# Weight sums of the second MLP product: started behind the first product's weight loads, and two of the four made by transfers that add

## The chip, the cores and the metric

One core of one Trainium2 chip. The metric is the device time of one execution in microseconds; the time of a kernel is the median of its runs. A profile shows one execution, whose own time is given beside its span.

## The reference

A hybrid decoder block on 512 tokens (and 16 meta tokens) of width 1024: two token mixers side by side (gated linear attention and an S5 state-space layer), merged by gates, and then an MLP with a squared ReLU. The change touches the MLP alone:

```python
hn = rmsnorm(h, g_ffn_pre[l])
f = jnp.square(jax.nn.relu(hn @ w_ff1[l])) @ w_ff2[l]
h = h + rmsnorm(f, g_ffn_post[l])
```

w_ff1 is 1024 x 4096 and w_ff2 is 4096 x 1024, in float32.

## The kernel before

Every matmul is made of three: a float32 operand is split into a high part (float32r, made by ACT at line 152, `whi`) and the rest (made by DVE at line 165, `wlo`), and hi x hi, hi x lo and lo x hi are summed in PSUM.

**First product.** w_ff1 is taken in 32 tiles of 128 columns. One tile is a 512 KB load on the SP queue (line 158, `wraw`, three buffers), a split into `whi` and `wlo` (three buffers each), 24 matmuls of 128x128 by 512 tokens into one PSUM bank of four, a ReLU by ACT (line 1251) and a square by DVE (line 1252) into `f`. The first three tiles are begun early and in two halves; the loop `for m in range(EARLY, MF)` runs over the other 29. After every fourth tile DVE makes sums of parts of `f` (`early_sums`).

**Second product.** It is done by a scheme with seven products of half size instead of eight (Strassen and Winograd's): sums of quarters of `f` are multiplied by quarters of w_ff2 or by sums of them. The four kinds of sums of w_ff2's quarters are made while the first product runs, in 16 steps, j = 0 to 15 (`weight_sums`). Step j loads 256 rows of w_ff2 (1 MB, `w2raw`, two buffers), makes four differences of 128x512 each on DVE into `w2t` (two buffers), and writes them (1 MB) to a tensor in HBM, `td2` (named t2d in the profile). Both transfers are issued by POOL. Call a step's two row blocks A and B, and their left and right halves l and r; then the four are

- t0 = Ar - Al
- t1 = Br - t0
- t2 = Br - Ar
- t3 = Bl - t1

The second product's sub-products read w_ff2 or td2 in 512 KB pieces on SP (line 1286) and begin when the first product is over; the second of them is the first that reads td2.

**Order.** A planner sets the order of the instructions in each engine's queue when the program is built, from the data dependences, the free buffers and a model of costs; at run time each queue is worked off in that order. `tc.issue_after(x)` makes the instructions of a block that are on x's engine come after x in that engine's queue; it adds no wait between engines. `behind()` is `issue_after` of the last load kept in `loaded`. In the stretch before the loop PE's order is the written one (`pinned`), in the loop it is the planner's.

Of the kernel before, what the change touches and what calls it, by code (L numbers as in the profile page):

```python
# [11 lines left out]
AF = mybir.ActivationFunctionType  # L12
ALU = mybir.AluOpType
# [3 lines left out]
P = 128  # L17
D = 1024
KT = D // P
SEQ = 512  # L20
# [8 lines left out]
MF = DFF // P  # L29
# [20 lines left out]
def hybrid_block(ctx: ExitStack, tc: tile.TileContext, io, out: bass.AP):  # L50
    nc = tc.nc
    V, S, G = nc.vector, nc.scalar, nc.gpsimd
# [18 lines left out]
    def mk(pool, shape, dt=F32, tag=None, **kw):  # L71
        count[0] += 1
        name = f"{tag or 'x'}_{count[0]}"
        size = 1
        for n in shape[1:]:
            size *= n
        if pool not in lined or size % LINE == 0:
            return pool.tile(shape, dt, tag=tag or name, name=name, **kw)
        t = pool.tile([shape[0], -(-size // LINE) * LINE], dt, tag=tag or name, name=name, **kw)[:, :size]
        if len(shape) == 2:  # L80
            return t
        dims = " ".join("abcd"[: len(shape) - 1])
        return t.rearrange(f"p ({dims}) -> p {dims}", **dict(zip("abcd", shape[1:])))

    def f32(t):
        return t.bitcast(F32)

    def pool(name, bufs=1, space=None, stack=None, side="left", padded=False):
        kw = {"side": side} if space is None else {"space": space}
        if space != DRAM:  # L90
            kw["reuse_waits"] = "tile"
        made = (stack or ctx).enter_context(tc.tile_pool(name=name, bufs=bufs, **kw))
        if padded:
            lined.append(made)
        return made
# [25 lines left out]
    def bank(tag="sm"):  # L121
        return mk(ps_mm if tag == "mm" else ps_sm, [P, 512], tag=tag)
# [28 lines left out]
    def split_hi(dst, src, scale=1.0):  # L151
        S.activation(dst, src, AF.Copy, scale=scale)  # L152

    def raw_w(src):

        kt, n = src.shape[0] // P, src.shape[1]
        raw = mk(wp, [P, kt, P], tag="wraw", bufs=3)
        return nc.sync.dma_start(raw[:, :, :n], src.rearrange("(k p) n -> p k n", p=P)), raw

    def split_w(raw):  # L160
        kt = raw.shape[1]
        hi = mk(wp, [P, kt, P], F32R, tag="whi", bufs=3)
        lo = mk(wp, [P, kt, P], F32R, tag="wlo", bufs=3)
        split_hi(hi, raw)
        V.tensor_sub(lo, raw, f32(hi))  # L165
        return hi, lo

    def load_w(src):

        return [split_w(raw_w(src[:, c : c + P])[1]) for c in range(0, src.shape[1], P)]  # L170

    def mm3(ps, whi, wlo, xhi, xlo, kt):

        for k in range(kt):
            PE.matmul(ps, whi(k), xhi(k), start=(k == 0), stop=False)
            PE.matmul(ps, whi(k), xlo(k), start=False, stop=False)
            last = PE.matmul(ps, wlo(k), xhi(k), start=False, stop=(k == kt - 1))
        return last

    def feat_tile(w, xh, xl, c0, c1, ps, m=P, kt=KT):  # L180
        hi, lo = w
        return mm3(ps, lambda k: hi[:, k, :m], lambda k: lo[:, k, :m], lambda k: xh[:, k, c0:c1], lambda k: xl[:, k, c0:c1], kt)
# [77 lines left out]
    loaded = None  # L260

    def behind():
        return tc.issue_after(loaded.ins) if loaded else ExitStack()

    def x_load(t):
        xt = mk(pxt, [P, D], tag="xt", bufs=5)
        xts.append((xt, P, t * P))
        return nc.sync.dma_start(xt, io["x"][0, t * P : (t + 1) * P, :])


    for kind, i in (("x", 0), ("x", 1), ("u", 0), ("x", 2), ("u", 1), ("x", 3)):
        with behind():
            if kind == "x":
                loaded = x_load(i)
            else:
                loaded, raw = raw_w(w_in[:, C_U + i * P : C_U + (i + 1) * P])
# [11 lines left out]
    for i in range(2):  # L288
        ps = bank()
# [5 lines left out]
    for i, (xt, n, col) in enumerate(xts):  # L295
        sq = mk(pxt, [P, D], tag="xsq", bufs=2)
        squared = S.activation(sq[:n], xt[:n], AF.Square, accum_out=ss[:n, i : i + 1])
# [18 lines left out]
    ps = bank()  # L316
# [781 lines left out]
    for c in range(0, D, 256):  # L1098
        ss_ = []
        for i, w in enumerate(load_w(wg[:, D + c : D + c + 256])):  # L1100
            m = c // P + i
            ps = bank("mm")
# [7 lines left out]
        for i, w in enumerate(load_w(wg[:, c : c + 256])):  # L1110
            m = c // P + i
            ps = bank("mm")
# [18 lines left out]
    for k in range(KT):  # L1131
        raw = mk(wp, [P, D], tag="wraw", bufs=3)
# [19 lines left out]
    hh = mk(pf, [P, KT, SEQ], F32R, tag="hh")  # L1152
    hl = mk(pf, [P, KT, SEQ], F32R, tag="hl")
# [48 lines left out]
    EARLY = 3  # L1202
    w1 = io["w_ff1"][0]
    w2 = io["w_ff2"][0]
# [10 lines left out]
    f = mk(pff, [P, MF, SEQ], tag="f")  # L1215
# [3 lines left out]
    NJ = MF // 2  # L1219
# [9 lines left out]
    def early_sums(jj):  # L1229

        a11, a12, a21, a22 = quarters(jj)
        V.tensor_add(s1[:, 2 * jj : 2 * jj + 2], a21, a22)
        V.tensor_sub(a21, a11, a21)

    spw = ExitStack()
    pw2 = pool("pw2", stack=spw)

    def weight_sums(j):

        raw = mk(pw2, [P, 2, D], tag="w2raw", bufs=2)  # L1240
        nc.gpsimd.dma_start(raw, w2[2 * j * P : (2 * j + 2) * P, :].rearrange("(k p) n -> p k n", p=P))  # L1241
        t_ = mk(pw2, [P, 4, 512], tag="w2t", bufs=2)
        V.tensor_sub(t_[:, 0], raw[:, 0, 512:], raw[:, 0, :512])  # L1243
        V.tensor_sub(t_[:, 1], raw[:, 1, 512:], t_[:, 0])  # L1244
        V.tensor_sub(t_[:, 2], raw[:, 1, 512:], raw[:, 0, 512:])  # L1245
        V.tensor_sub(t_[:, 3], raw[:, 1, :512], t_[:, 1])  # L1246
        nc.gpsimd.dma_start(td2[:, j].rearrange("i p n -> p i n"), t_)  # L1247

    def relu2(m, ps):
        r_ = mk(pff, [P, SEQ], tag="relu", bufs=2)  # L1250
        S.activation(r_, ps, AF.Relu)
        V.tensor_mul(f[:, m], r_, r_)

    for w, ps in zip(ws, pss):
        feat_tile(w, hh, hl, 256, 512, ps[:, 256:])
    pinned[0] = False
    for m, ps in enumerate(pss):
        relu2(m, ps)
    for m in range(EARLY, MF):
        ps = bank("mm")  # L1260
        feat_tile(load_w(w1[:, m * P : (m + 1) * P])[0], hh, hl, 0, SEQ, ps)
        relu2(m, ps)
        if m % 4 == 3:
            early_sums(m // 4)
        if m % 2 == 0:
            weight_sums(m // 2 - 2)
    for j in (NJ - 2, NJ - 1):
        weight_sums(j)
    spw.close()
    sf.close()  # L1270

# [137 lines left out]
```

## Time and profile before

| | |
|---|---|
| median of 3 runs | 909.98 us (909.49 to 912.02) |
| profiled execution | 909.35 us, span 907.6 us |
| granted TensorE clock | 0.996 of full speed |
| PE busy | 888.8 us, 98% of the span |
| DVE busy | 669.0 us, 74% |
| ACT busy | 407.6 us, 45% |
| POOL busy | 85.2 us, 9% |
| loop over the first product's 29 tiles | 585.4 to 746.8 us of the span |
| weight sums: first load issued, last write issued | 569.9 us, 696.0 us |

In the profile, a line such as "676.93 0.69 DVE L1243 TENSOR_TENSOR w2t<-w2raw ..." gives the start, the duration, the engine, the line of the kernel, the operation and the tiles written and read; in brackets stands how long the engine sat idle before it, and what ended that. A row of the busy time by stage gives the stretch, its length, the busy time of PE, PE's weight loads, DVE, ACT and POOL with their instructions in parentheses, the granted clock, the mean busy share of the 16 DMA engines, and GB/s. A row of a DMA queue gives its packets, MB, and the time of its packets as a share of the 16 engines' time. "DMA to landing" is the time from a transfer's issue to its end.

### The profile page before, as it was taken

To read this page: it belongs to the slowest core of one execution; us is meant where nothing else is said; L and a number is where in the kernel's file an instruction comes from. 1 tells how busy PE (TensorE), PEld (TensorE's weight loads), DVE (VectorE), ACT (ScalarE), POOL (GpSimd) and SP (SyncE) were. 2 spreads that over 40 slices of the span, in tenths; PEclk is the share of its full clock that TensorE was granted. 3 is DMA by queue.
4 is the path that set the end of the run, shared out by engine and by line. 5 is a ranking of instruction groups with operands and counts; after the bars stand their busy time and mean duration, and the time that the engine had idled before them with its cause. 6 is when DMAs were issued, how large, how long until landed. Compare 5 with 4: busy or idle time off the path is not lost.

```text
span 907.6 us, 13464 instructions
## 1 busy us (share of the span) xinstructions
PE 888.8 (98%) x4980; PEld 759.2 (84%) x4980; DVE 669.0 (74%) x1203; ACT 407.6 (45%) x667; POOL 85.2 (9%) x160
## 2 busy tenths in 40 slices
PE   7999999999999999999999999999999999999996
PEld 5899899898988888888888888988877888888885
DVE  7779998877877699876344765667766348778786
ACT  6362355556563434224223544432322326665762
POOL 1311100010101201103000000111120000000000
PEclk9999999999999999999999999999999999999999
DMA  7733644344435536367654672599999437655564
GB/s 231 184 107 120 198 107 116 101 122 113 109 105 141 159 100 193 107 193 261 185 152 148 215 191 70 180 358 377 392 377 320 128 100 272 208 188 202 167 209 139
DMA packets 172147, 166.68 MB, mean 184 GB/s; under 512 B 22397, under 2 KB 137153, under 8 KB 172082
## 3 DMA queue, kind: packets, MB, share of 16 engines
q1 hardware_dynamic: 155920, 110.48, 41.7%
q0 software_dynamic: 14480, 50.56, 14.8%
q10 hardware_dynamic: 1682, 4.79, 1.6%
q8 instruction: 39, 0.64, 0.3%
q14 instruction: 26, 0.21, 0.1%
HBM read 131.42 MB, written 34.37 MB: 183 GB/s over the span
## 4 chain that ended last, share of the span: by engine, by line
PE 83%; DMA 7%; issue 4%; DVE 4%; POOL 1%; ACT 0%; DVEq 0%; POOLq 0%
PE mm L60 59%; PE sm L60 21%; DMA w2raw<-in_w_ff_dram 6%; PE sm L65 3%; DVE xl L193 1%; DVE xn L302 0%; DVE w2t L1243 0%; POOL t2d L1247 0%; DMA xt<-in_x_dram 0%; DVE w2t L1244 0%; DVE wlo L165 0%; DVE w2t L1246 0%; DVE c L1352 0%; POOL w2raw L1241 0%; DVE w2t L1245 0%
## 5 line engine op out<-in xcount | busy, mean ns | idle before, releaser
L152 ACT ACTIVATE whi<-wraw 128x1024 fp32r<-128x1024 f32 x160 | 168.5, 1056 | 242.6 <-PE mm L60 174.7
L60 PE MATMUL mm<-xh,whi 128*128 128x512 f32 (+2 forms) x544 | 184.1, 338 | 0.5 <-DVE xl L193 0.5
L60 PE MATMUL mm<-xl,whi 128*128 128x512 f32 (+2 forms) x544 | 180.0, 331 | 0.5 <-DVE xl L193 0.5
L60 PE MATMUL mm<-xh,wlo 128*128 128x512 f32 (+2 forms) x544 | 180.0, 331 | 0.0
L165 DVE TENSOR_TENSOR wlo<-wraw,whi 128x1024 fp32r<-128x1024 f32 x104 | 126.9, 1221 | 56.5 <-ACT whi L152 51.8
L60 PEld LDWEIGHTS mm<-xh,whi 128*128 128x128 f32 x544 | 104.2, 192 | 11.3 <-issue 1.2
L60 PEld LDWEIGHTS mm<-xl,whi 128*128 128x128 f32 x544 | 104.2, 192 | 9.2 <-DVE xl L193 0.8
L60 PEld LDWEIGHTS mm<-xh,wlo 128*128 128x128 f32 x544 | 104.1, 191 | 9.1
L60 PE MATMUL mm<-hh,wlo 128*128 128x512 f32 (+1 forms) x280 | 104.3, 373 | 2.5 <-DVE wlo L165 2.5
L60 PE MATMUL mm<-hh,whi 128*128 128x512 f32 (+1 forms) x280 | 104.1, 372 | 0.2 <-ACT hh L152 0.2
L60 PE MATMUL mm<-hl,whi 128*128 128x512 f32 (+1 forms) x280 | 104.0, 371 | 0.3 <-DVE hl L193 0.3
L1289 DVE TENSOR_TENSOR wlo<-wraw,whi 128x1024 fp32r<-128x1024 f32 x56 | 68.4, 1222 | 23.0 <-ACT whi L152 23.0
L60 PE MATMUL sm<-wlo,fh 128*128 128x512 f32 x192 | 74.8, 390 | 0.0
L60 PE MATMUL sm<-whi,fh 128*128 128x512 f32 x192 | 74.7, 389 | 0.0
L60 PE MATMUL sm<-whi,fl 128*128 128x512 f32 x192 | 74.7, 389 | 0.0
L60 PEld LDWEIGHTS mm<-hh,wlo 128*128 128x128 f32 x280 | 52.7, 188 | 13.0 <-DVE wlo L165 4.1
L60 PEld LDWEIGHTS mm<-hl,whi 128*128 128x128 f32 x280 | 52.7, 188 | 9.7 <-DVE hl L193 0.5
L60 PEld LDWEIGHTS mm<-hh,whi 128*128 128x128 f32 x280 | 52.7, 188 | 9.4 <-ACT hh L152 0.5
L152 ACT ACTIVATE fh<-f 128x512 fp32r<-128x512 f32 x48 | 30.1, 629 | 44.0 <-PE sm L60 25.9
L60 PE MATMUL mm<-gl,whi 128*128 128x512 f32 x128 | 49.8, 389 | 0.0
L60 PE MATMUL mm<-gh,whi 128*128 128x512 f32 x128 | 49.8, 389 | 0.0
L60 PE MATMUL mm<-gh,wlo 128*128 128x512 f32 x128 | 49.8, 389 | 0.0
(409 smaller groups left out, 1562.1 us busy)
## 6 DMA issues: line engine op xcount, KB each, us to landing
wraw<-in_w_ff_dram SPq DMA_DIRECT2D x56, 512.0 KB, 4.9
wraw<-in_w_in_dram SPq DMA_DIRECT2D x48, 512.0 KB, 4.2
w2raw<-in_w_ff_dram POOLq DMA_DIRECT2D x16, 1024.0 KB, 9.6
t2d<-w2t POOLq DMA_DIRECT2D x16, 1024.0 KB, 7.5
wraw<-t2d SPq DMA_DIRECT2D x32, 512.0 KB, 3.7
wraw<-in_w_glu_dram SPq DMA_DIRECT2D x16, 512.0 KB, 3.8
M<-kpad SPq DMA_DIRECT2D x64, 64.0 KB, 2.5
wraw<-in_w_o_gla_dram SPq DMA_DIRECT2D x8, 512.0 KB, 4.5
```

The lines of the kernel that those rows point to most:

```text
L60: ins = nc.tensor.matmul(*args, **kw)
L65: ins = nc.tensor.transpose(*args, **kw)
L152: S.activation(dst, src, AF.Copy, scale=scale)
L165: V.tensor_sub(lo, raw, f32(hi))
L193: V.tensor_sub(lo[:, dst, col : col + n], pv[:, :, :n], f32(hi)[:, dst, col : col + n])
L1289: V.tensor_sub(bl, raw, f32(bh))
```

## The change

- Step j's load of w_ff2 rows moves from POOL's queue to SP's, and stands there behind the load of a tile of w_ff1: tile 3 + floor(28 j / 16), so that the 16 steps are spread over tiles 3 to 29. Before, they were written every second tile, and the planner ran them as their buffers came free.
- t0 and t2 are no longer made by DVE. ACT writes -Al and -Ar (copies with a scale of -1), and a transfer issued by POOL adds Ar and Br to them, read from w_ff2 in HBM a second time (512 KB).
- t1 and t3 stay on DVE, and are put behind the squaring of the tile that follows; the write to td2 follows them. Step j is a generator: its first part ends at `yield`, its second part is run one tile later.
- `w2t` has three buffers instead of two. `relu2` returns its last instruction, so that others can be put behind it.

```diff
     def weight_sums(j):
         raw = mk(pw2, [P, 2, D], tag="w2raw", bufs=2)
-        nc.gpsimd.dma_start(raw, w2[2 * j * P : (2 * j + 2) * P, :].rearrange("(k p) n -> p k n", p=P))
-        t_ = mk(pw2, [P, 4, 512], tag="w2t", bufs=2)
-        V.tensor_sub(t_[:, 0], raw[:, 0, 512:], raw[:, 0, :512])
+        rows = w2[2 * j * P : (2 * j + 2) * P, :].rearrange("(k p) n -> p k n", p=P)
+        nc.sync.dma_start(raw, rows)
+        t_ = mk(pw2, [P, 4, 512], tag="w2t", bufs=3)
+
+        S.activation(t_[:, 0], raw[:, 0, :512], AF.Copy, scale=-1.0)
+        S.activation(t_[:, 2], raw[:, 0, 512:], AF.Copy, scale=-1.0)
+        nc.gpsimd.dma_start(t_[:, 0:4:2], rows[:, :, 512:], accum_op=ALU.add)
+        yield
         V.tensor_sub(t_[:, 1], raw[:, 1, 512:], t_[:, 0])
-        V.tensor_sub(t_[:, 2], raw[:, 1, 512:], raw[:, 0, 512:])
         V.tensor_sub(t_[:, 3], raw[:, 1, :512], t_[:, 1])
         nc.gpsimd.dma_start(td2[:, j].rearrange("i p n -> p i n"), t_)
...
+    j, begun = 0, []
     for m in range(EARLY, MF):
         ps = bank("mm")
-        feat_tile(load_w(w1[:, m * P : (m + 1) * P])[0], hh, hl, 0, SEQ, ps)
-        relu2(m, ps)
+        loaded, raw = raw_w(w1[:, m * P : (m + 1) * P])
+        w = split_w(raw)
+        feat_tile(w, hh, hl, 0, SEQ, ps)
+        squared = relu2(m, ps)
         if m % 4 == 3:
             early_sums(m // 4)
-        if m % 2 == 0:
-            weight_sums(m // 2 - 2)
-    for j in (NJ - 2, NJ - 1):
-        weight_sums(j)
+        for part in begun:
+            with tc.issue_after(squared.ins):
+                next(part, None)
+        begun = []
+
+        while j < NJ and EARLY + j * (MF - EARLY - 1) // NJ <= m:
+            with behind():
+                begun.append(weight_sums(j))
+                next(begun[-1])
+            j += 1
+    for part in begun:
+        next(part, None)
```

More of the change, by code (lines that the diff above doesn't have):

```diff
@@ L1251, in relu2 @@
         S.activation(r_, ps, AF.Relu)
-        V.tensor_mul(f[:, m], r_, r_)
+        return V.tensor_mul(f[:, m], r_, r_)
     for w, ps in zip(ws, pss):
```

## The prediction

> **What bounds the kernel now.** I read the page's share of engines first, then the waits of PE in the stretch of the change (575 to 750 us), then busy time by stage, then the timeline around PE's gaps, then the POOL queue.
>
> ```profile
> PE 888.8 (98%) x4980; PEld 759.2 (84%) x4980; DVE 669.0 (74%) x1203; ACT 407.6 (45%) x667; POOL 85.2 (9%) x160
> ...
> PE mm L60 <- DVE wlo L165: 2.5, 3, 1.0
> ...
> 585.00:665.00 80.00, 80.00 (x356) 66.31 (x356) 58.74 (x85) 23.41 (x31) 16.14 (x22) 1.00 1.02 367
> 665.00:690.00 25.00, 22.49 (x96) 17.38 (x95) 17.14 (x25) 6.19 (x8) 5.18 (x7) 1.00 1.03 370
> 690.00:746.00 56.00, 56.00 (x249) 46.37 (x248) 28.02 (x34) 16.99 (x22) 0.76 (x1) 1.00 0.49 153
> ```
>
> PE is the bound, and it stalls in this stage at one place only: between 665 and 690 us it is busy for 22.49 of 25.00 us. There the DMA engines are full (share 1.03), as they have been since 585 us; afterwards they are half idle (0.49). The granted clock is 1.00 throughout. So the most that this edit can win is what these stalls cost. Two matmuls of one kind, 24 apart, give the undisturbed tile; the first matmul of the loop over the first product's tiles and the first of the second product give the stage.
>
> ```profile
> 639.85 0.39 PE L60 MATMUL mm<-hh,whi 128*128 128x512 f32 x1
> 645.29 0.39 PE L60 MATMUL mm<-hh,whi 128*128 128x512 f32 x1
> ...
> 585.42 0.40 PE L60 MATMUL mm<-hh,whi 128*128 128x512 f32 x1
> 746.84 0.39 PE L60 MATMUL sm<-whi,fh 128*128 128x512 f32 x1
> ```
>
> A tile takes 5.44 us, so 29 tiles take 157.8 us; they took 746.84 - 585.42 = 161.4 us. The stage loses **3.7 us** (2.5 us as waits, the rest as slower matmuls just behind each gap). Now what PE waits for:
>
> ```profile
> 676.93 0.69 DVE L1243 TENSOR_TENSOR w2t<-w2raw 128x512 f32<-128x512 f32 x1 [2.35 <-DMA w2raw<-in_w_ff_dram]
> 677.54 0.69 DVE L1245 TENSOR_TENSOR w2t<-w2raw 128x512 f32<-128x512 f32 x1
> 678.14 0.68 DVE L1244 TENSOR_TENSOR w2t<-w2raw,w2t 128x512 f32<-128x512 f32 x1
> 678.86 0.69 DVE L1246 TENSOR_TENSOR w2t<-w2raw,w2t 128x512 f32<-128x512 f32 x1
> 679.47 1.22 DVE L165 TENSOR_TENSOR wlo<-wraw,whi 128x1024 fp32r<-128x1024 f32 x1
> ...
> 680.74 0.50 PE L60 MATMUL mm<-hh,wlo 128*128 128x512 f32 x1 [0.95 <-DVE wlo L165]
> ```
>
> DVE waits for a weight-sum load (w2raw), does its four sums, and only then the low half (wlo) of the tile for which PE stands still. The order of DVE's queue is fixed, so a late weight-sum load holds up the first product.
>
> How late comes from a loop of two buffers: the load for sum j+2 cannot start before sum j's last subtraction frees its w2raw.
>
> ```profile
> 666.65 0.78 POOL L1247 DMA_DIRECT2D t2d<-w2t  x1 [7.16 <-DVE w2t L1246]
> 667.42 0.70 POOL L1241 DMA_DIRECT2D w2raw<-in_w_ff_dram  x1
> 673.14 0.78 POOL L1247 DMA_DIRECT2D t2d<-w2t  x1 [5.03 <-DVE w2t L1246]
> ...
> 679.85 0.78 POOL L1247 DMA_DIRECT2D t2d<-w2t  x1 [5.24 <-DVE w2t L1246]
> ```
>
> From 666.65 to 679.85 one turn takes 13.2 us (write issued, load issued 0.77 us later, 9.5 us to the first subtraction, 2.6 us of subtractions, hand-over), hence 6.6 us per sum. The queue order has about one sum per 5.44 us tile here, so DVE falls behind by about 1.2 us per sum until its lead is gone. That lead is worked out from how early the next weights are split when nothing disturbs:
>
> ```profile
> 730.49 1.06 ACT L152 ACTIVATE whi<-wraw 128x1024 fp32r<-128x1024 f32 x1 [3.90 <-PE mm L60]
> ```
>
> With three buffers the split of tile m+3 starts when tile m ends, and takes 1.06 us here and 1.22 us on DVE; PE needs it two tiles (10.9 us) later. Lead: 10.9 - 2.3 = 8.6 us, or some seven sums at 1.2 us each, which is about where the stall at 667 to 687 us lies.
>
> **The change, part by part.**
>
> *Pacing.* Sum j now starts behind the load of tile 3 + 28j/16, so there are 16 sums in 28 tiles: one in 1.75 tiles, 9.5 us, and a turn of two buffers may last 19.0 us where it now takes 13.2. The closing subtractions come behind the squaring of the following tile. Last sum: tile 29, closed behind tile 30 (about 743 us), written by some 752 us. Its readers:
>
> ```profile
> L1286 SPq DMA_DIRECT2D wraw<-t2d x12: 359/360/367, 759.8 to 787.8; - x12
> ```
>
> The first read (759.8 us) wants sums 0 and 1, the last pair is read much later: nothing is late there.
>
> *The new turn.* Taken out: two of four subtractions (0.6 us apart, 1.2 us) and the load's place behind the write on POOL (0.77 us, against 0.36 us of issue on SP, the row just above: 0.4 us). Put in: two ACT copies, one more POOL issue (0.78 us, rows above), and the adding transfer's time to landing, A. The nearest copy:
>
> ```profile
> L152 ACT ACTIVATE fh<-f 128x512 fp32r<-128x512 f32 x48 | 30.1, 629 | 44.0 <-PE sm L60 25.9
> w2raw<-in_w_ff_dram POOLq DMA_DIRECT2D x16, 1024.0 KB, 9.6
> t2d<-w2t POOLq DMA_DIRECT2D x16, 1024.0 KB, 7.5
> DMA to landing us min/median/max: 6.0/9.6/11.6
> DMA to landing us min/median/max: 3.8/7.9/14.6
> ```
>
> (The last two rows are from the views of tile w2raw and of line 158, the first product's loads of 512 KB.) Two copies: 1.3 us. New turn: 13.2 - 1.2 - 0.4 + 1.3 + 0.8 + A = 13.7 + A if the load still needs 9.5 us, and 10.2 + A if it lands in the least time seen, 6.0 us. It now shares no queue with the 1 MB write ahead of it, and sums come at 9.5 instead of 6.6 us; against that it stands behind 512 KB loads on SP. I take the middle, 11.9 + A.
>
> No transfer of before adds. Bounds for A: 512 KB plain and undisturbed, 3.8 us; twice the bytes under load, 7.5 to 9.6 us. I take 5.6 us, the middle of 3.8 and 7.5, since the bytes are nearest to the former and the load on the engines to the latter. Turn: 17.5 us, below 19.0: DVE no longer falls behind and PE's waits go, **-3.7 us**. At A = 3.8 the turn has 3.3 us to spare and the gain is the same; it cannot be more. At A = 9.6 the turn is 21.5 us: 1.25 us per sum, over 14 sums 17.5 us, less the lead of 8.6: 8.9 us of stalls, a net +5.2 us. With 13.7 + 9.6 = 23.3 us it is 2.1 x 14 - 8.6 = 21 us of stalls, net +17.
>
> The Trainium skill (Collectives: The Full Stack, "The bandwidth ceiling: the fold count and why AG ≠ RS ≠ AR") says that an adding DMA issues two source reads per piece written, so that a reduce runs at about half the speed of a copy. By that rule the 512 KB would be priced as 1 MB, 7.5 us by the write's row, and the turn 19.4 us: 0.2 x 14 = 3 us of lag, inside the lead, so the same forecast with nothing to spare. No run so far shows it.
>
> *The engines' total.* Rates come from stretches in which one queue dominates: the software queue in 620 to 640 us, the hardware queue in 700 to 720 us.
>
> ```profile
> q0 software_dynamic: 1544, 5.94, 77.5%
> ...
> q1 hardware_dynamic: 6236, 3.14, 53.9%
> ...
> 569.89 0.72 POOL L1241 DMA_DIRECT2D w2raw<-in_w_ff_dram  x1
> ```
>
> 15.5 us for 5.94 MB is 2.6 us per MB; 10.8 us for 3.14 MB is 3.4. Per tile: 0.52 MB of first-product weights, 1.8 us; 4/7 of a sum's load and of its write, 1.6 us each; 4/7 of an adding transfer, 0.8 us, or 1.6 if its two addends, both of which must be read, count in full. That is 5.8 to 6.6 us per 5.44 us tile, or 1.07 to 1.21 against the 1.02 to 1.03 sustained in the windows above. So for the length of the sums the engines are at or over their limit. But sums may drift: at most 26 x 1.8 + 16 x (2.7 + 2.7 + 1.4 to 2.7) = 156 to 177 us of transfers stand against the 177 us from 570 us (where the first sum loads start now) to 747. It fits, at the upper price with no spare.
>
> *Edits hidden at nothing.* ACT gains 32 x 0.63 = 20 us on a stage in which it is busy for 47 of 161 us; a copy that waits for its load holds up the split and relu queued behind it, covered by the same lead. DVE loses 32 x 0.6 = 19 us. On SP the sum's load waits for its buffer with later w1 loads behind it; these are issued up to five tiles ahead of use (three raw buffers on top of two split tiles), 27 us, so a wait of a few us costs nothing until that is gone. POOL's write of sum j can delay the adding issue of j+1 queued behind it; it was busy 22 of 161 us. The third w2t buffer takes space, not time.
>
> **Rivals.**
>
> *The adding transfer is dear (slower).* The mechanism is the turn above; all other steps go as told. It decides at A = 8.9 us: turn 20.8, 0.9 x 14 - 8.6 = 4 us lost, as much as the gain. At 9.6 us it gives 915, at 10 us 918 (1.45 x 14 - 8.6 = 12 lost), and with the upper ends of both bounds some 927. What speaks for it are two rows of the first product's loads, the first in 660 to 680 us, the second in 700 to 720 us:
>
> ```profile
> DMA to landing us min/median/max: 10.3/10.4/10.5
> ...
> DMA to landing us min/median/max: 3.8/4.0/7.1
> ```
>
> Beside full engines 512 KB slow from 4.0 to 10.4 us, and the engines will be at 1.07 or more. Against it: these are loads in short pieces on the hardware queue, while POOL's own writes of 1 MB landed in 7.5 us under the same load, and adding transfers go through POOL.
>
> *The wait only changes its name (same).* DVE waits for the adding transfer instead of the load, and first-product loads still land late: they keep 1 to 4 us of stalls somewhere in the 161 us. Time 907.5 to 911. For: a DMA share near 1 over the whole stage, where before it was free from 700 us on. Against: the turn has 1.5 us to spare at my A.
>
> *Nothing is paced (same).* The edge behind w1's load is empty where the buffer's wait is later anyway; then sums run as fast as the turn lets them. 910. The closing subtractions behind the squaring speak against it.
>
> **How the numbers follow.** The profiled execution took 909.35 us (span 907.6), 0.6 below the median of the runs, 909.98. Less 3.7 the profile gives 905.7 and the median **906.3**. About 0.3% (2.7 us) is what a measurement here tells from no change, so full recovery just clears it. Chances: stalls gone 0.47; a new name or no pacing 0.20; dear adding transfer 0.33. The likeliest alone: 905.2 to 907.2. The range reaches up to 918, an A of 10 us, leaving out the upper part of the dear case.
>
> **What would show it.** Right: no PE wait for wlo in 575 to 750 us, the second product starting at 743 us, DMA share in 690 to 746 us near 1, writes to t2d 9.5 us apart up to 750. Step by step: the adding issue's time to landing against 5.6 and 8.9 us; DVE's waits at its closing subtractions; the sum's load against 6.0 to 9.5 us. Wrong: a row with DVE or ACT waiting for the adding transfer over 4 us a time, and PE gaps from 660 us on.

## The result, and the profile after

The changed kernel takes **952.99 us** (median of 4 runs, 948.23 to 954.58) against 911.0 us of the kernel before beside it (909.49 to 912.1): a ratio of **1.0444**, 95% interval 1.0409 to 1.048. It is slower by 42 us; 906.3 was forecast, with 918 as the upper end. The profiled execution took 954.58 us, its span is 952.8 us.

The page of the changed kernel: engines, and the issues of the weight sums (KB each, median us to landing).

```profile
PE 909.3 (95%) x4980; PEld 766.6 (80%) x4980; DVE 650.5 (68%) x1171; ACT 423.6 (44%) x699; POOL 93.8 (10%) x160
...
w2raw<-in_w_ff_dram SPq DMA_DIRECT2D x16, 1024.0 KB, 8.6
t2d<-w2t POOLq DMA_DIRECT2D x16, 1024.0 KB, 10.0
...
w2t<-in_w_ff_dram POOLq DMA_DIRECT2D x16, 512.0 KB, 6.1
```

DVE lost 32 instructions and ACT gained 32, as the change says. PE has as many matmuls as before and is 95% busy instead of 98. The adding transfer lands in 6.1 us, where 5.6 was forecast and 8.9 was the point of no gain. Next, the first matmul of the loop and the first of the second product, from PE's timeline:

```profile
589.04 0.40 PE L60 MATMUL mm<-hh,whi 128*128 128x512 f32 x1
...
788.94 0.39 PE L60 MATMUL sm<-whi,fh 128*128 128x512 f32 x1
```

The stage lasts 199.9 us instead of 161.4, against 157.8 undisturbed. Of 45.2 us between the spans (952.8 and 907.6) 38.5 lie in it, 3.1 behind it (163.9 instead of 160.8 us from its end to the span's), and 3.6 ahead of it, where the two programs are alike: over all kernels below it begins between 584.1 and 589.0 us. Start-to-start distances of PE's matmuls in the stage, each less the usual 0.227 us, split the loss: distances over 0.8 us hold 27.4 us (17 gaps; 3.0 before), those of 0.25 to 0.8 us hold 14.3 (68 of them; 0.5 before). Together 38.2 us more than before.

Who waited, in 560 to 800 us of the changed kernel (us in total, times, longest):

```profile
ACT w2t L1245 <- DMA w2raw<-in_w_ff_dram: 120.1, 14, 10.8
DVE wlo L165 <- ACT whi L152: 115.4, 20, 9.6
...
PE mm L60 <- ACT whi L152: 20.6, 10, 4.1
...
PE mm L60 <- DVE wlo L165: 4.5, 9, 0.5
...
DVE w2t L1249 <- DMA w2t<-in_w_ff_dram: 0.8, 2, 0.6
```

Read it from PE upwards: PE waits for whi on ACT; ACT stands for 120 us in front of the first copy, waiting for the 1 MB load, with the splits of the first product queued behind. Hardly anything waits for the adding transfer (0.8 us). One turn in the timelines of ACT, DVE and SP:

```profile
679.06 0.37 SPq L1242 DMA_DIRECT2D w2raw<-in_w_ff_dram  x1
...
688.02 0.63 ACT L1245 ACTIVATE w2t<-w2raw 128x512 f32<-128x512 f32 x1 [10.26 <-DMA w2raw<-in_w_ff_dram]
688.56 0.61 ACT L1246 ACTIVATE w2t<-w2raw 128x512 f32<-128x512 f32 x1
689.08 1.04 ACT L152 ACTIVATE whi<-wraw 128x1024 fp32r<-128x1024 f32 x1
690.03 0.58 ACT L1255 ACTIVATE relu<-mm 128x512 f32<-128x512 f32 x1
...
691.29 0.68 DVE L1256 TENSOR_TENSOR f<-relu 128x512 f32<-128x512 f32 x1
691.90 0.69 DVE L1249 TENSOR_TENSOR w2t<-w2raw,w2t 128x512 f32<-128x512 f32 x1
692.62 0.69 DVE L1250 TENSOR_TENSOR w2t<-w2raw,w2t 128x512 f32<-128x512 f32 x1
...
693.34 0.37 SPq L1242 DMA_DIRECT2D w2raw<-in_w_ff_dram  x1
```

This is a **ring through four queues**. The load for sum j starts when the closing subtractions of sum j-2 free its buffer. The copies of j wait for it; the ReLU of a tile whose matmuls are done stands behind them on ACT; its square, and behind the square the closing of sum j-1, wait for that ReLU; and that closing frees the buffer for the load of j+1. So in most turns only one load is in flight in spite of two buffers, and one turn makes *one* sum: 693.34 - 679.06 = 14.3 us here, 9.0 of it load. In the written order of the queues one tile, 5.4 us, lies between the square that frees a buffer and the copies that need its load, and the load takes 8.6. Over the stage the writes to td2 go from 604.47 to 789.58 us: 15 steps of 12.3 us, where one in 9.5 us was forecast, from a turn able to make one in 8.75 (half of 17.5). All 16 sums end with the stage.

### The profile page after: what moved, and what is told of

Same layout as the page of the kernel before. It is cut to its first block, busy times and chain, and to the rows that moved or that the text cites. A ratio compares the mean times of both kernels' runs of the same rounds, so it can differ in the third digit from the quotient of the medians.

```text
span 952.8 us, 13532 instructions
## 1 busy us (share of the span) xinstructions
PE 909.3 (95%) x4980; PEld 766.6 (80%) x4980; DVE 650.5 (68%) x1171; ACT 423.6 (44%) x699; POOL 93.8 (10%) x160
## 4 chain that ended last, share of the span: by engine, by line
PE 76%; DMA 10%; issue 5%; DVE 5%; ACT 2%; POOL 0%; ACTq 0%; DVEq 0%; POOLq 0%
PE mm L60 55%; PE sm L60 19%; DMA w2raw<-in_w_ff_dram 8%; PE sm L65 3%; DMA wraw<-in_w_ff_dram 2%; ACT whi L152 1%; DVE wlo L165 1%; DMA w2t<-in_w_ff_dram 1%; DVE w2t L1249 1%; DVE w2t L1250 1%; DVE f L1256 1%; ACT w2t L1246 1%; DVE xl L193 0%; DVE xn L302 0%; DVE wlo L1304 0%
## 5 line engine op out<-in xcount | busy, mean ns | idle before, releaser
L60 PE MATMUL mm<-hh,whi 128*128 128x512 f32 (+1 forms) x280 | 109.6, 391 | 20.8 <-ACT whi L152 20.6
L60 PE MATMUL mm<-hh,wlo 128*128 128x512 f32 (+1 forms) x280 | 109.2, 390 | 4.8 <-DVE wlo L165 4.5
L60 PE MATMUL mm<-hl,whi 128*128 128x512 f32 (+1 forms) x280 | 107.7, 385 | 0.3 <-DVE hl L193 0.3
L60 PEld LDWEIGHTS mm<-hh,whi 128*128 128x128 f32 x280 | 55.0, 197 | 34.6 <-ACT whi L152 25.1
L60 PEld LDWEIGHTS mm<-hh,wlo 128*128 128x128 f32 x280 | 54.9, 196 | 20.5 <-DVE wlo L165 11.0
L60 PEld LDWEIGHTS mm<-hl,whi 128*128 128x128 f32 x280 | 55.3, 198 | 10.2 <-DVE hl L193 0.5
L1245 ACT ACTIVATE w2t<-w2raw 128x512 f32<-128x512 f32 x16 | 10.1, 630 | 120.1 <-DMA w2raw<-in_w_ff_dram 120.1
```

The lines of the kernel that those rows point to most:

```text
L60: ins = nc.tensor.matmul(*args, **kw)
L1245: S.activation(t_[:, 0], raw[:, 0, :512], AF.Copy, scale=-1.0)
```

## The experiments

The expectations set three explanations against each other. Theory A: the loss is waiting in the ring. Rival B: the adding transfers are dear, in the DMA engines' time above all. Rival C: the 1 MB loads on SP stand in the way of the first product's loads.

**Is it the pacing? (e4_pace, e8_pace24)** Pacing, the load on SP and the yield stay; all four differences are DVE's again, in the closing part. e8 also spreads the sums over 24 tiles instead of 28.

```diff
-        S.activation(t_[:, 0], raw[:, 0, :512], AF.Copy, scale=-1.0)
-        S.activation(t_[:, 2], raw[:, 0, 512:], AF.Copy, scale=-1.0)
-        nc.gpsimd.dma_start(t_[:, 0:4:2], rows[:, :, 512:], accum_op=ALU.add)
         yield
+        V.tensor_sub(t_[:, 0], raw[:, 0, 512:], raw[:, 0, :512])
         V.tensor_sub(t_[:, 1], raw[:, 1, 512:], t_[:, 0])
+        V.tensor_sub(t_[:, 2], raw[:, 1, 512:], raw[:, 0, 512:])
...
-        while j < NJ and EARLY + j * (MF - EARLY - 1) // NJ <= m:
+        while j < NJ and EARLY + j * (MF - EARLY - 5) // NJ <= m:   # e8 alone
```

> The pacing alone: loads on SP behind the first product's loads and the closing part one tile later as in the changed kernel, but all four sums on DVE in that closing part, with no copies on ACT and no adding transfers. Theory A: nothing on ACT waits for these loads, DVE's turn has time to spare, and the stalls of the kernel before go too: 905 to 908 us. Rival B: also 905 to 908. Rival C: 915 or more, with ACT waiting for the first product's loads.

> The pacing alone (all four sums on DVE), with the 16 sums spread over 24 tiles in place of 28, so that the last is written four tiles before the second product. With 28 tiles the first product lost nothing (157.8 us for 29 tiles), but the second lost 1.3 us just after its start, where its loads met the last sums. Theory A: both go, 904.5 to 907 us. Rival C (loads on SP get in the way as soon as the pace rises): first-product loads land late and 1 to 3 us come back, 907 to 911.

e4: 907.83 us, ratio 0.9983 [0.9968, 0.9998]. e8: 905.96 us, ratio **0.9957 [0.9941, 0.9972]**, the fastest of all and faster than both kernels. In both the stage takes exactly 157.8 us. Busy time by stage of e4:

```profile
585.00:665.00 80.00, 80.00 (x364) 66.61 (x363) 54.21 (x73) 25.93 (x35) 5.30 (x7) 1.00 0.84 278
665.00:746.00 81.00, 81.00 (x359) 67.09 (x358) 52.89 (x73) 22.75 (x30) 6.77 (x9) 1.00 0.91 303
```

PE is busy without a break, clock 1.00, engines below 1. In the stage, pacing with the loads on SP does what was forecast. Behind it e4 loses 1.4 us (162.2 us instead of 160.8 from its end to the span's), e8 nothing.

**Is it the adding? (e7_adds)** The kernel before, unpaced, with its load on POOL, but with the two copies, the adding transfer and three w2t buffers:

```diff
-        V.tensor_sub(t_[:, 0], raw[:, 0, 512:], raw[:, 0, :512])
+        S.activation(t_[:, 0], raw[:, 0, :512], AF.Copy, scale=-1.0)
+        S.activation(t_[:, 2], raw[:, 0, 512:], AF.Copy, scale=-1.0)
+        nc.gpsimd.dma_start(t_[:, 0:4:2], rows[:, :, 512:], accum_op=ALU.add)
         V.tensor_sub(t_[:, 1], raw[:, 1, 512:], t_[:, 0])
-        V.tensor_sub(t_[:, 2], raw[:, 1, 512:], raw[:, 0, 512:])
```

> The adding transfers alone, on the kernel before: loads on POOL at the planner's pace, copies on ACT, adding transfers on POOL, three w2t buffers, no pacing. Copies stand two or three tiles after the freeing, 16 sums in 24 tiles. Theory A: the planner's pace of 8.2 us per sum is below what a turn with an adding transfer needs (some 20 us per two sums), so the lead is used up: 912 to 930 us. Rival B: 940 or more, as in the changed kernel. If the pacing were what costs, 905 to 909.

943.17 us, 1.0361 [1.0327, 1.0395]: the second half of the change alone costs 33 us, more than theory A had. The waits in 560 to 800 us:

```profile
ACT w2t L1243 <- DMA w2raw<-in_w_ff_dram: 90.2, 12, 13.2
...
DVE w2t L1247 <- DMA w2t<-in_w_ff_dram: 43.7, 12, 7.2
```

Without pacing, too, ACT waits for the load most of all, and DVE here for the add as well.

**Does the add set the turn? (e3_copy, e10_tinyadd)** The order of every queue stays as in the changed kernel; in e3 the transfer is plain (the addition is left out), in e10 it adds 8 of 512 columns (the rest of t0 and t2 is left out).

```diff
-        nc.gpsimd.dma_start(t_[:, 0:4:2], rows[:, :, 512:], accum_op=ALU.add)
+        nc.gpsimd.dma_start(t_[:, 0:4:2], rows[:, :, 512:])                              # e3
+        nc.gpsimd.dma_start(t_[:, 0:4:2, :8], rows[:, :, 512:520], accum_op=ALU.add)     # e10
```

> The changed kernel with the adding transfer replaced by a plain one of the same 512 KB to the same place (the addition is left out, so two of the four sums lack their negated part). Theory A: 945 to 955 us, since DVE waited only 0.8 us in total for the adding transfer; its landing falls from 6.1 to 4 or 5 us. Rival B: the time falls to 905 to 920. Rival C: 945 to 955.

> The changed kernel, its adding transfers cut from 512 to 8 columns of each half (the rest of the addition is left out); the order on every engine is that of the changed kernel. Theory A: the turn hangs on the load, not on the add: 940 to 955 us. Rival B: some 40 us of engine time go: 905 to 920.

e3: 958.31 us, e10: 942.85 us (one run each). The first row is e3's wait, the second its stretch 665 to 746 us, the third e10's wait:

```profile
ACT w2t L1245 <- DMA w2raw<-in_w_ff_dram: 128.6, 14, 13.0
...
665.00:746.00 81.00, 65.47 (x241) 50.60 (x242) 27.17 (x35) 23.62 (x36) 8.84 (x12) 0.87 0.79 260
```

```profile
ACT w2t L1245 <- DMA w2raw<-in_w_ff_dram: 113.3, 14, 11.2
```

With a transfer that lands in 4.0 us (e3), and with nearly none (e10), ACT waits just as long for the load. In e3 PE loses 15 of 81 us while the engines are 0.79 busy: this is waiting in queues, not want of bandwidth. It costs some 33 us by itself (e10, beside 909.47 of the kernel before). Why e3 is even above the changed kernel, and above its expectation (its load landed in 10.5 us, not 8.6), stays open.

**Which wait of the ring can be opened? (e1_raw3, e6_nogate, e5_late, e2_negpool)** e1 gives w2raw three buffers (and w2t two, for space; all queues but SP's keep their order). e6 leaves away the order behind the square. e5 puts the copies one tile later, behind a ReLU, and the closing one tile after them. e2 makes the copies on POOL.

```diff
-        raw = mk(pw2, [P, 2, D], tag="w2raw", bufs=2)
+        raw = mk(pw2, [P, 2, D], tag="w2raw", bufs=3)      # e1; w2t: bufs=2
...
-            with tc.issue_after(squared.ins):              # e6
-                next(part, None)
+            next(part, None)
...
         nc.sync.dma_start(raw, rows)
+        yield                                              # e5
...
-        for part in begun:
+        for part in copied:                                # e5
             with tc.issue_after(squared.ins):
                 next(part, None)
+        for part in begun:
+            with tc.issue_after(relued[0].ins):
+                next(part)
+        copied, begun = begun, []
...
-        S.activation(t_[:, 0], raw[:, 0, :512], AF.Copy, scale=-1.0)   # e2, t_[:, 2] likewise
+        G.tensor_scalar(t_[:, 0], raw[:, 0, :512], -1.0, None, op0=ALU.mult)
```

> The changed kernel with three w2raw buffers and two w2t buffers in place of two and three; the order of the instructions on PE, DVE, ACT and POOL is the same, on SP the weight-sum loads stand earlier. Theory A (a ring through ACT): in the changed kernel ACT's two copies of one sum stand ahead of a ReLU whose squaring gates the closing subtractions of the sum before, and only these free the buffer for the next load, so every sum waits for a whole load of 8.6 us and takes some 14 us. A third buffer starts each load one sum earlier: ACT's waits for w2raw fall from 120 us to under 25, PE's gaps go, 905 to 916 us. Rival B (the adding transfers are dear for the DMA engines): the same bytes and the same adds, 945 to 955. Rival C (the 1 MB loads on SP stand in the way of the first product's loads): 945 or more, since they are issued earlier still.

> The changed kernel without the edge that puts the closing subtractions behind the square of the following tile; the planner then puts them where it likes, two tiles after the copies, and the copies come one to three tiles (2.1 on average) after the freeing. Theory A: about a third of the copies still wait for a whole load, 912 to 930 us. Rival B: 945 or more, the same transfers in less time.

> The changed kernel with the two ACT copies and the adding transfer one tile later (copies behind the ReLU of the tile after the load, closing subtractions behind the square of the tile after that); same engines, transfers, buffers and bytes. In ACT's queue there are then two or three tiles (10.9 to 16.3 us) between the square that frees a buffer and the copies that need its next load, where the changed kernel has one tile (5.4 us) for a load of 8.6 us. Theory A (one tile between freeing and copies): ACT's waits for w2raw fall from 120 to under 30 us, PE's gaps go, 905 to 914 us. Rival B (the adding transfers are dear): 925 or more, with DVE waiting for them 4 us or more a time.

> The changed kernel with the two negated copies on POOL in place of ACT; nothing else moves. Theory A: ACT waits for no weight-sum load any more, so splits and ReLUs come on time and the squaring with them; 905 to 916 us, with POOL waiting instead. Rival B (adding transfers dear): 945 to 955, DVE or POOL waiting for them. Rival C (loads on SP): 945 to 955, ACT waiting for the first product's loads.

e1: 953.88 us, 1.0484 [1.0455, 1.0513]. e6: 969.55 us (one run). e5: 950.38 us, 1.0438 [1.0407, 1.0469]. e2: 930.2 us, 1.0228 [1.0202, 1.0255]. All four are misses of theory A as it was put. The waits in 560 to 800 us, of e1, then e6, e5 and e2:

```profile
ACT w2t L1245 <- issue: 61.0, 5, 13.3
ACT w2t L1245 <- DMA t2d<-w2t: 59.0, 7, 13.7
```

```profile
ACT w2t L1245 <- DMA w2raw<-in_w_ff_dram: 122.0, 14, 13.4
DVE w2t L1249 <- DMA w2t<-in_w_ff_dram: 81.0, 12, 11.8
...
PE mm L60 <- DVE wlo L165: 42.8, 12, 9.2
```

```profile
DVE w2t L1250 <- DMA w2t<-in_w_ff_dram: 59.1, 11, 9.5
ACT w2t L1246 <- DMA w2raw<-in_w_ff_dram: 57.6, 14, 6.8
ACT whi L152 <- DMA wraw<-in_w_ff_dram: 48.7, 14, 7.9
```

```profile
ACT whi L152 <- DMA wraw<-in_w_ff_dram: 73.7, 16, 9.7
...
DVE w2t L1249 <- DMA w2t<-in_w_ff_dram: 47.1, 7, 10.4
```

In e1 the copies wait at the same place for as long (120.0 us), now for the buffer of w2t: its write of two sums earlier takes 10.3 us and is issued behind the closing, so the ring closes through the other tile. (The first row names no transfer, but its five waits, too, end 9.6 to 11.8 us after POOL issued such a write.) Three buffers of both tiles were not run. In e6 ACT waits for the load as before (122.0 us); the closing, now early in DVE's queue, waits for the add on top, with low halves that PE needs behind it (42.8 us). In e5 the wait is shared out between load, add and first product. So an edge taken out alone leaves the wait or hands it on. Only e2, where ACT's queue holds no copy, wins 23 us; its loss has a new first row: the *first product's* weights come late from the DMA engines.

**The engines' time alone (e9_idle_add, e13_idle_paced)** e4 with an adding transfer of the same size into a scratch tile that nobody reads; in e13 it is issued behind its sum's write (w2t has two buffers in both, for space).

```diff
+    idle = mk(pw2, [P, 2, 2, 512], tag="idle")
+    G.memset(idle, 0.0)
...
+        nc.gpsimd.dma_start(idle[:, j % 2], rows[:, :, 512:], accum_op=ALU.add)        # e9
         nc.gpsimd.dma_start(td2[:, j].rearrange("i p n -> p i n"), t_)
...
-        nc.gpsimd.dma_start(td2[:, j].rearrange("i p n -> p i n"), t_)                 # e13
+        written = nc.gpsimd.dma_start(td2[:, j].rearrange("i p n -> p i n"), t_)
+        with tc.issue_after(written.ins):
+            nc.gpsimd.dma_start(idle[:, j % 2], rows[:, :, 512:], accum_op=ALU.add)
```

> The pacing alone over 28 tiles (all four sums on DVE, as in the run that gave 907.8), plus the same 16 adding transfers of 512 KB on POOL, into a scratch tile that nobody reads; w2t has two buffers to make room. The DMA engines do all that they do in the changed kernel and nobody waits for an add. Theory A (waiting: each sum's legs stand one tile apart in the queues, where a leg lasts 8 to 10 us): 905 to 911 us. Rival B (the engines' time: an add costs double and the engines are full): 930 to 955, with first-product loads landing late.

> The pacing alone over 28 tiles, with 16 adding transfers of 512 KB into a scratch tile that nobody reads, each issued by POOL just behind the write of its sum, so spread over the whole stage. If the engines' time is a cause by itself (rival B), 915 to 926 us, with DMA share at 1.0 or more and first-product loads late; if all of the loss is waiting for the sums' legs (theory A), 906 to 911.

e9: 924.32 us, 1.0159 [1.0136, 1.0182], between what theory A and rival B had, but not clean: without an order the adds ran in a row, POOL's writes stood behind them, and PE lost 14.4 us in one gap. e13: 929.48 us, 1.0201 [1.018, 1.0222], 21.7 us over e4 and a little over what I expected. A wait and the stretch 665 to 705 us of e13:

```profile
ACT whi L152 <- DMA wraw<-in_w_ff_dram: 111.5, 20, 16.2
...
665.00:705.00 40.00, 40.00 (x177) 33.11 (x178) 28.28 (x39) 10.79 (x14) 8.12 (x9) 1.00 1.08 346
```

No sum waits for an add here, and still the first product's weights are late: the engines stand at 1.08, where e4 had 0.98, and move 346 GB/s, less than e15 below at 1.04. From 600 to 740 us these 512 KB loads land in 12.6 us in the median, in e4 in 8.3. The engines' time need not be all of it: SP stood for 85.6 us of 560 to 800 us in front of the sums' loads, with first-product loads queued behind (e4: 60.4), and what that added isn't told apart.

**Both opened (e12_loose, e11_late_copy, e15_loose_copy, e14_loose24)** e12: w2raw in two tiles of [P, D], two buffers each, two loads; copies one tile after the load behind a ReLU, closing two tiles after the copies behind a square. e15 is e12, and e11 is e5, with a plain transfer (the addition left out; all queues in the same order). e14 is e12 over 24 tiles.

```diff
+        rawa = mk(pw2, [P, D], tag="w2rawa", bufs=2)
+        rawb = mk(pw2, [P, D], tag="w2rawb", bufs=2)
+        nc.sync.dma_start(rawa, rows[:, 0])
+        nc.sync.dma_start(rawb, rows[:, 1])
+        yield
...
+        for part in waiting:
             with tc.issue_after(squared.ins):
                 next(part, None)
+        for part in begun:
+            with tc.issue_after(relued[0].ins):
+                next(part)
+        waiting, copied, begun = copied, begun, []
```

> The changed kernel's pace, adds and bytes, with every leg given room: w2raw split in two tiles (the half that ACT copies, freed by the copies; the half for the closing subtractions, freed by these), copies behind the ReLU one tile after the load, closing subtractions behind the square two tiles after the copies. The second half's next load and the copies' buffers have 3.25 to 3.5 tiles a turn (17.7 to 19 us). Theory A: no leg of 6 to 10 us is waited for, 905 to 914 us. Rival B: the engines have the same work in the same time, 930 to 955, with DMA share at 1 or more and first-product loads late.

> The kernel with copies and adds one tile later, with plain transfers in place of the adding ones (the addition is left out); the order on every engine is the same. There the add's leg has one tile (5.4 us) and it landed in 10.6. Theory A: a plain transfer lands in 4 to 6 us, so that leg closes nearly, 910 to 930. Rival B: some 20 us of engine time go, 920 to 935. If neither, it stays at 950.

> The loosened kernel with plain transfers in place of the adding ones (the addition is left out); the order on every engine is the same. If the second read of the add is what fills the engines: 908 to 914 us, and the transfers land in 4 to 6 us rather than 9.4. If the 512 KB themselves are too much: 920 to 925.

> The loosened kernel with its 16 sums over 24 tiles in place of 28, so that they end earlier but need a higher rate of the engines. If its loss came from the late end alone: 908 to 915 us. If the engines are full (they were at 1.06 to 1.08 of share from 625 us on): 922 to 940, the stalls moving into the first product.

e12: 925.08 us, 1.0166 [1.0148, 1.0184], between what theory A and rival B had. e11: 929.81 us, 20.6 below e5. e15: 910.11 us beside 911.2 of the kernel before. e14: 924.7 us, 1.0144 [1.0113, 1.0174]. (e11 and e15 are one run each; their plain transfers landed in 7.8 and 7.7 us, not in the 4 to 6 expected.) The software queue's share of the 16 engines in the whole span, of e4, e15 and e12:

```profile
q0 software_dynamic: 10128, 33.78, 9.7%
```

```profile
q0 software_dynamic: 12432, 42.17, 12.3%
...
665.00:705.00 40.00, 40.00 (x178) 33.15 (x177) 20.46 (x26) 15.81 (x23) 6.69 (x9) 1.00 1.04 368
```

```profile
q0 software_dynamic: 14480, 42.17, 14.5%
...
665.00:705.00 40.00, 40.00 (x178) 33.12 (x177) 19.25 (x24) 15.08 (x22) 7.95 (x8) 1.00 1.07 330
```

Times the spans (907.1, 908.4, 923.4 us) these are 88.0, 111.7 and 133.9 us of all 16 engines. Sixteen plain transfers of 512 KB take 23.7 us of them, **1.48 us each**; sixteen adding ones of the same size take 45.9, **2.87 us each, 1.94 times as much** (1.9 to 2.0, as the shares are rounded). The Trainium skill's rule that the prediction weighed (Collectives: The Full Stack, "The bandwidth ceiling: the fold count and why AG ≠ RS ≠ AR": an adding DMA reads two sources, stated there for collectives) is borne out in engine time, by these 1.94. Single packets agree: in e12's trace an adding packet of 2048 bytes takes 176 ns in the median, a plain one of 2048 bytes (on the hardware queue) 84, a plain one of 4096 bytes 159. So it isn't just that the adding transfers come in smaller packets.

e15 holds all that the change adds, copies, extra transfer and pacing, and loses nothing in the stage (157.8 us), though 5.3 us behind it (166.1). Adding in place of copying, with all else alike, makes it 15 us slower (e12). A share over 1 is not a loss by itself: e15 stands at 1.04 from 625 to 705 us. e12, at 1.08 and 1.07 there, moves 339 and 330 GB/s where e15 moves 372 and 368, and from 600 to 740 us the first product's loads land in 12.6 us in the median instead of 8.4.

e15 beside e3 is also the plainest test of the ring: the same plain transfers at the same pace take 958.31 us in the tight order and 910.11 in the loose one (in e15 the loads are cut in two as well). In e14 the loss only moves from the second product's beginning (e12: stage 163.3, rest 174.8 us) into the first (172.5 and 161.9): ending earlier doesn't help.

## Why the prediction was wrong

*Right.* PE's 3.7 us of stalls and their cause: with pacing and the load on SP they are gone to the last (e4, e8). The load's 8.6 us on SP lie in the forecast 6.0 to 9.5, and the add's 6.1 us to landing is near 5.6, but with the DMA engines at 0.91 over the stage: in e12, where they stand at 1.06 to 1.08 from 625 to 746 us, it is 9.4. SP's queue did no harm in the stage (e4). That nothing would be late behind it held for e8 alone.

*Wrong, and decisive: "a copy that waits for its load holds up the split and relu queued behind it, covered by the same lead".* The lead, 8.6 us, covers one such wait. The changed kernel has 14 of them, 8.6 us each on the mean (120.1 / 14), and the ring returns one with nearly every sum. The prediction's other half of the same mistake is "The new turn": it added the legs of a turn as if two sums ran freely side by side, 11.9 + A for two, and never asked which instruction of *another* sum or tile stands ahead of each leg in its queue. The measured turn is 12.3 us for one. The working did name what a waiting copy holds up, "the split and relu queued behind it", but not that this queue leads back to the next load.

*Wrong, second: "It fits, at the upper price with no spare".* The upper price was the right one, 2.7 us for a transfer against 2.87 measured. But a total that just fits is not free. With no sum waiting for the adds it costs 21.7 us (e13), and 15 us with everything loose (e12 over e15): the first product's 512 KB loads are what comes late, 111.5 us of ACT's waiting in e13. The row of 10.4 us that the prediction set against itself pointed there.

*Not in the sum: the restart.* 14.3 us of the stage are matmuls that follow slowly behind a gap, 10.9 of them while PE's clock was granted at half (below).

*The rivals.* "The adding transfer is dear" had the right sign, not the mechanism: A stayed below its point of 8.9 us, and DVE waited 0.8 us for it. "Nothing is paced" is refuted by e4. "The wait only changes its name" had a wait that moves, but to DVE and the adding transfer, for 1 to 4 us; it moved to ACT and the load, for 42.

*The account.* Pacing brings 1.4 us (e4), 4.2 over 24 tiles (e8). The ring costs about 33 us with next to no adding (e10), adding in place of copying or of nothing 15 to 22 us (e12 over e15, e13 over e4). These don't add up one by one: together they make 42. A likely reason, not shown, is that a kernel that waits leaves the DMA engines free. From loose to tight order the step is 28 us with adding transfers (e12 to the changed kernel) and 48 with plain ones (e15 to e3), though the loads of e12 and e15 are also cut in two. The kernel before, run beside each experiment, lay between 909.2 and 911.2 us, so differences between experiments are good to some 2 us.

## What to carry to other kernels

Before an instruction that waits for a transfer is put into an in-order queue, follow the queue onward: if what stands behind it leads, over other engines, to what frees that transfer's buffer, there is a ring, and each turn costs a whole transfer in spite of two buffers; a third of one tile alone need not open it (e1). Work moved from an engine to the DMA engines is paid in their time, an adding transfer about twice by its bytes; here, with their busy share near 1, the price came back on the first product's loads. Test the halves of a change apart: here one half was a small gain (e8), the other most of the loss (33 of 42 us, e7).

## What the runs showed of the hardware

**The clock falls behind short gaps.** PE's timeline in the changed kernel:

```profile
671.42 0.39 PE L60 MATMUL mm<-hh,wlo 128*128 128x512 f32 x1
675.90 0.74 PE L60 MATMUL mm<-hh,whi 128*128 128x512 f32 x1 [4.10 <-ACT whi L152]
...
677.76 0.63 PE L60 MATMUL mm<-hh,whi 128*128 128x512 f32 x1
678.18 0.63 PE L60 MATMUL mm<-hl,whi 128*128 128x512 f32 x1
678.61 0.63 PE L60 MATMUL mm<-hh,wlo 128*128 128x512 f32 x1
679.04 0.57 PE L60 MATMUL mm<-hh,whi 128*128 128x512 f32 x1
...
679.68 0.40 PE L60 MATMUL mm<-hh,wlo 128*128 128x512 f32 x1
679.91 0.40 PE L60 MATMUL mm<-hh,whi 128*128 128x512 f32 x1
```

After 4.1 us of idling the matmuls start 0.43 us apart instead of 0.23, until 679.04, 3.1 us after the restart. Busy time by stage has the granted clock in the third column from the end:

```profile
652.10:655.50 3.40, 3.25 (x7) 2.07 (x8) 3.40 (x6) 1.71 (x3) 0.33 (x1) 0.50 0.72 107
676.00:679.40 3.40, 3.30 (x7) 2.17 (x8) 3.37 (x5) 1.76 (x3) 0.48 (x2) 0.50 0.68 92
704.30:720.30 16.00, 13.16 (x54) 10.00 (x55) 9.15 (x12) 4.43 (x7) 3.27 (x4) 1.00 0.93 291
```

In the stage the trace has the clock at half in six stretches, from 652.1, 676.0, 720.4, 730.6, 757.9 and 781.8 us, five of 3.4 us and one (757.9) of 6.8, 23.9 us in all; in before's stage it has none. Of the 68 slow distances 47 lie in them and hold 10.9 of the 14.3 us; the other 21, at full clock, hold 3.4. The Trainium skill (TensorE: Matmul & The Clock Gate, "Part 1: The HAM clock gate") gives 426.7 ns for this size on a cold array and an idle window of about 3.4 us; the trace agrees on 0.43 us, and here with the window too; but the half clock also follows a distance of only 2.22 us between two starts (from 649.73, the first row), and doesn't follow one of 2.53 (from 701.76, the last row).

**Adding on the way.** Beside 1.94 times the engine time, an adding 512 KB landed in 6.1 us where the plain one in the same order took 4.0 (e3), and in 9.4 where it took 7.7 (e12, e15). POOL spent 1.21 us on its issue in the median instead of 0.71 (e3); with 8 columns it was 1.21 as well (e10), so the bytes don't set it. An adding issue and a plain one, of 1 MB, in the changed kernel:

```profile
689.47 1.17 POOL L1247 DMA_DIRECT2D w2t<-in_w_ff_dram  x1 [9.32 <-ACT w2t L1246]
693.62 0.81 POOL L1251 DMA_DIRECT2D t2d<-w2t  x1 [2.98 <-DVE w2t L1250]
```

Loads of 512 KB on the hardware queue land later beside busy engines: in 10.4 us in before's 660 to 680 us (share 1.03), in 9.4 in the median of the changed kernel's 600 to 780 us (0.91 over the stage), in 4.0 in before's 700 to 720 us (0.49 around it).
